# Weighing of heads, casts and last sums of the attention layer, in another order

## The chip, the cores and the metric

The kernel runs on one core of a Trainium2 chip. The metric is the device time of one execution in microseconds. Engines are named as in the profile: PE is TensorE (products), DVE is VectorE, ACT is ScalarE, POOL is GpSimd, SP is SyncE, whose queue issues the DMA transfers.

## The reference

One sequence of 1024 rows by 1024 columns goes through an mLSTM layer and then through a layer of dilated attention; the second one is what the change touches. Cut to that:

```python
def dilated_attention_layer(x, w_in, w_out, kv_blocks, slopes):
    proj = x @ w_in                                   # queries of 3 groups, 8 heads of 128; gate z
    for g, (window, dilation) in enumerate(GROUPS_B): # (128,1), (512,4), (2048,16)
        o, lse = dilated_block_attention(qb, kb, vb, dilation, window // dilation, slopes)
        ...
    wts = jax.nn.softmax(jnp.stack(lses), axis=0)     # over the three groups
    o = jnp.sum(wts[..., None] * jnp.stack(outs), axis=0)
    y = o * jax.nn.silu(z)
    return y @ w_out

x = layer_norm(ALPHA * x + y, ln_g, ln_b)
```

All is float32. A product is made of three products of a reduced type: each operand is split into a high part h and the rest l, and h·h, h·l and l·h are summed.

## The kernel before, in words

`split` (lines 91 to 93) makes such a pair: ScalarE casts the high part (92), VectorE subtracts it for the rest (93). `mm3` (95 to 99) issues the three products (97, 98, 99), each of 128x128 by 128x512. A scheduler orders each engine's instructions by a model of their times, in which the order of the text is a priority; within `issue_after(ins)` an instruction may not be issued ahead of `ins`. Each engine works through its own queue in order and waits by semaphores for the others. SBUF is cut into numbered slots (s0 to s52) of 128x1024, PSUM into eight banks (b0 to b7) of 128x512. How many buffers a small tile gets is decided by the compiler's own placement.

The attention layer runs two quads of four heads, in each the three groups, in each the four heads: `queries_keys` (products by Strassen's scheme, sums on VectorE in 224, 230, 260, 261), `scores` (1260, 1269 maximum, 1271 its negative, 1273 Exp on ScalarE), `attend` (1287 transposes, 1341 products with the values, 1349 copies). In the third group `factors` and `merge` (1383 to 1403) turn the three groups' maxima and denominators into weights, written to memory (df). `fetch` starts the loads of a head's three outputs and weights (1411 to 1415); `combine` multiplies and sums them (1424, 1426) and multiplies with the gate (1428). `weigh` calls it for a head, pinned behind the last `split`, and writes the result y. Before, head h is weighed after the attention of the next head. The last gates (`gates(3)`, 1473 and 1474) follow behind head 7's attention, and then heads 6 and 7's y.

The output projection has eight blocks c of 128 columns of y and rows of w_out; for each, y and w_out are loaded (1544, 1546) and split, blocks 6 and 7 straight from heads 6 and 7. `block` (line 1557 on) sums one block into a bank: a row tile tb of 128 rows has two halves dm, each 24 products in one bank. Tiles 0 to 3 are summed together; then tiles 4 to 7 one by one in banks b0 to b7, two each. `begin` loads the residual rows (1565) and, in `add_rows` (937 to 941), adds them to a bank (940) and takes statistics (941) half by half. `finish` aggregates (928, 930), computes the reciprocal root by an integer guess (357, 359) and three Newton steps of three instructions (361 to 363), the bias (1580), normalises on ScalarE (1582), and multiplies and adds gain and shift on VectorE (1583, 1584). `finish_last`, for tiles 6 and 7, centres and multiplies with the gain (1594) while no root is needed yet, and then multiplies with the root and adds the shift (1597); tile 7 does both in halves, and stores each half.

At the start, `setup` loads three gate weights in_wifr (449) into slot 51, one after another, and GpSimd multiplies and sums each (424 to 426); ScalarE copies the result (454).

## Time and profile before

| | us |
|---|---|
| three runs | 2020.54, 2025.85, 2025.57 |
| median of the three | 2025.57 |
| profiled execution, its own time | 2023.8 |
| its span, first to last instruction | 2022.0 |
| TensorE busy | 1969.0 (97%) |
| VectorE busy | 1451.8 (72%) |
| ScalarE busy | 1010.7 (50%) |
| GpSimd busy | 154.0 (8%) |

The profile is one execution. The span is what its instructions take from the first to the last; 1.8 us lie around it. The mean granted clock of TensorE over it is 0.996 of 2.4 GHz.

### The profile page before, as it was taken

To read this page: it belongs to the slowest core of one execution; us is meant where nothing else is said; L and a number is where in the kernel's file an instruction comes from. 1 tells how busy PE (TensorE), PEld (TensorE's weight loads), DVE (VectorE), ACT (ScalarE), POOL (GpSimd) and SP (SyncE) were. 2 spreads that over 40 slices of the span, in tenths; PEclk is the share of its full clock that TensorE was granted. 3 is DMA by queue.
4 is the path that set the end of the run, shared out by engine and by line. 5 is a ranking of instruction groups with operands and counts; after the bars stand their busy time and mean duration, and the time that the engine had idled before them with its cause. 6 is when DMAs were issued, how large, how long until landed. Compare 5 with 4: busy or idle time off the path is not lost. (4 is left out here: it accounts for less than half of the span.)

```text
span 2022.0 us, 26727 instructions
## 1 busy us (share of the span) xinstructions
PE 1969.0 (97%) x9576; PEld 1631.2 (81%) x9576; DVE 1451.8 (72%) x2867; ACT 1010.7 (50%) x2008; POOL 154.0 (8%) x127
## 2 busy tenths in 40 slices
PE   8999999999999999999999999999999999999897
PEld 6778888788888888878788888878877888888686
DVE  8778787675577776457867765776679877757878
ACT  5455555535645543343524542565554566765531
POOL 0110000012145343000000000000000000000000
PEclk9999999999999999999999999999999999999999
DMA  4345465456754543516121143224156322123753
GB/s 169 138 162 198 160 221 181 148 166 222 280 203 163 192 163 117 183 62 231 52 73 63 53 146 105 84 84 146 64 210 210 115 94 84 63 84 108 261 199 125
DMA packets 113148, 292.26 MB, mean 145 GB/s; under 512 B 13236, under 2 KB 31092, under 8 KB 113016
## 3 DMA queue, kind: packets, MB, share of 16 engines
q1 hardware_dynamic: 113016, 290.56, 41.1%
q8 instruction: 75, 1.23, 0.3%
q14 instruction: 57, 0.47, 0.1%
HBM read 202.13 MB, written 88.39 MB: 144 GB/s over the span
## 5 line engine op out<-in xcount | busy, mean ns | idle before, releaser
L98 PE MATMUL b<-s,s 128*128 128x512 f32 (+3 forms) x2720 | 1035.5, 382 | 3.0 <-DVE s L93 3.0
L97 PE MATMUL b<-s,s 128*128 128x512 f32 (+2 forms) x2720 | 1010.6, 386 | 28.0 <-ACT s L92 18.6
L99 PE MATMUL b<-s,s 128*128 128x512 f32 (+3 forms) x2720 | 1023.0, 383 | 4.9 <-DVE s L93 4.5
L92 ACT CAST s<-s 128x512 fp32r<-128x512 f32 (+3 forms) x706 | 436.5, 638 | 544.9 <-PE b L99 276.0
L93 DVE TENSOR_TENSOR s<-s,s 128x512 fp32r<-128x512 f32 (+3 forms) x702 | 508.2, 739 | 276.2 <-ACT s L92 272.6
L97 PEld LDWEIGHTS b<-s,s 128*128 128x128 f32 x2720 | 511.9, 188 | 134.6 <-ACT s L92 27.6
L99 PEld LDWEIGHTS b<-s,s 128*128 128x128 f32 x2720 | 511.1, 188 | 105.7 <-DVE s L93 10.2
L98 PEld LDWEIGHTS b<-s,s 128*128 128x128 f32 x2720 | 512.8, 189 | 99.3 <-DVE s L93 5.2
L230 DVE TENSOR_TENSOR s<-s,b 128x512 f32<-128x512 f32 x144 | 98.1, 682 | 37.8 <-PE b L99 35.6
L1273 ACT ACTIVATE s<-s,nmax 128x128 f32<-128x128 f32 (+1 forms) x192 | 84.3, 441 | 27.7 <-DVE nmax L1271 27.5
L224 DVE TENSOR_TENSOR s<-s,b 128x512 f32<-128x512 f32 x96 | 65.1, 680 | 19.9 <-PE b L99 16.4
L93 DVE TENSOR_TENSOR s<-b,s 128x512 fp32r<-128x512 f32 (+1 forms) x96 | 51.7, 553 | 33.9 <-ACT s L92 30.0
L558 DVE SCALAR_TENSOR_TENSOR s<-s,c_convw,s 128x512 f32<-128x512 f32 (+3 forms) x96 | 71.4, 755 | 3.1 <-ACT s L555 2.8
L802 ACT ACTIVATE s<-s,k 128x128 f32<-128x128 f32 x144 | 47.2, 392 | 42.2 <-DVE s L93 18.7
L243 DVE TENSOR_TENSOR s<-s,s 128x512 f32<-128x512 f32 x48 | 33.0, 688 | 42.9 <-DMA s<-in_w_xm 15.1
L1269 DVE CUSTOM_DVE_ANT_0 s<-b,k 128x128 f32<-128x128 f32 (+1 forms) x192 | 57.2, 346 | 3.5 <-PE b L99 3.2
L92 ACT CAST s<-b 128x512 fp32r<-128x512 f32 (+1 forms) x96 | 43.9, 480 | 21.9 <-PE b L99 14.5
L310 DVE TENSOR_TENSOR s<-s,s 128x1024 f32<-128x1024 f32 x32 | 40.1, 1253 | 20.1 <-DMA s<-in_w_o 9.9
L314 DVE TENSOR_TENSOR s<-s,b 128x512 f32<-128x512 f32 x80 | 50.7, 680 | 5.0 <-PE b L99 3.7
L1220 DVE SCALAR_TENSOR_TENSOR s<-s,s 128x512 fp32r<-128x512 f32 x48 | 42.3, 883 | 10.1 <-ACT s L1219 9.6
L761 POOL TENSOR_TENSOR s<-s 128x512 fp32r<-128x512 f32 x32 | 43.4, 1369 | 76.3 <-ACT s L760 68.8
L1287 PE MATMUL b<-c_ident,s 128*128 128x128 f32 x280 | 46.3, 277 | 2.0 <-ACT s L1273 1.9
(185 smaller groups left out, 1527.9 us busy)
## 6 DMA issues: line engine op xcount, KB each, us to landing
s<-in_w_qk SPq DMA_DIRECT2D x48, 512.0 KB
s<-in_w_out SPq DMA_DIRECT2D x40, 512.0 KB
dp<-s SPq DMA_DIRECT2D x32, 512.0 KB
s<-dp SPq DMA_DIRECT2D x32, 512.0 KB
s<-in_w_z SPq DMA_DIRECT2D x24, 512.0 KB
s<-in_w_v SPq DMA_DIRECT2D x24, 512.0 KB
dg<-s SPq DMA_DIRECT2D x24, 512.0 KB
s<-dg SPq DMA_DIRECT2D x24, 512.0 KB
```

What stands on the lines that cost most here:

```text
L92: self.nc.scalar.copy(h, src)
L93: self.last_split = (l_eng or self.nc.vector).tensor_tensor(l, src, f(h), op=ALU.subtract)
L97: mm(ps, lh, rh, start=start, stop=False, skip_group_check=skip)
L98: mm(ps, lh, rl, start=False, stop=False, skip_group_check=skip)
L99: mm(ps, ll, rh, start=False, stop=stop, skip_group_check=skip)
L224: V.tensor_tensor(o, p, q, op=add)
L230: V.tensor_tensor(o, p[lane][rows], q[lane][rows], op=add)
L314: V.tensor_tensor(o, p, q, op=add)
L558: V.scalar_tensor_tensor(u[i][:, lo:o + 512], xm[i][:, lo - s:o + 512 - s], convw[:, c, 3 - s:4 - s], u[i][:, lo:o + 512], op0=ALU.mult, o ...
L802: A.activation(E[:, i * P:i * P + P], src[:, i * P:i * P + P], AF.Exp, bias=self.bias[:, hd, ig, j:j + 1])
L1269: V.tensor_tensor_reduce(out=dst, in0=sc, in1=bias, op0=ALU.add, op1=ALU.max, scale=1.0, scalar=-3e38, accum_out=mx[:, b:b + 1])
L1273: self.last_exp = A.activation(res[b][0], res[b][0], AF.Exp, bias=nm[:, b:b + 1], accum_out=stat[:, 1, g, b:b + 1])
```

## The change

Three parts. **Weighing:** `weigh` is called from the middle of a `queries_keys` (or of `gates`) two heads later, behind the first of its steps, instead of after the next head's attention; heads 6 and 7's order behind a maximum or a split is written anew, and the slots of the sums are the same ring for both quads. **Casts:** the splits of the output projection's w_out and y (blocks 0 to 5 of y, all of w_out) may not issue ahead of the last Exp. **Last tiles:** the add of the second half of tiles 5, 6 and 7 may not issue ahead of the last VectorE operation of the tile before; tile 7's first half is centred on ScalarE (with a bias, minus the mean) and multiplied with the gain on GpSimd, instead of both on VectorE.

```diff
-    def add_rows(self, r, bs, ps, dm):
+    def add_rows(self, r, bs, ps, dm, behind=None):
...
-        V.scalar_tensor_tensor(r[:, ds], r[:, ds], ALPHA, ps, op0=ALU.mult, op1=ALU.add)
+        with self.tc.issue_after(behind.ins) if behind else ExitStack():
+            V.scalar_tensor_tensor(r[:, ds], r[:, ds], ALPHA, ps, op0=ALU.mult, op1=ALU.add)
...
-            self.strassen(self.quarters(a["w_qk"][g, h]), x, ones, None, done, V)
+            for n, _ in enumerate(self.strassen_steps(self.quarters(a["w_qk"][g, h]), x, ones, None, done, V)):
+                if n == 1:
+                    amid(h)
...
-        def weigh(h, fetched):
-
-            with self.tc.issue_after(self.last_split.ins):
+        def weigh(h, fetched, behind):
+
+            with self.tc.issue_after(behind.ins):
                 acc = combine(*fetched)
...
+        def weigh_late(h):
+
+            nonlocal late, merged, fourth
+            if not late or late[0] > h - 2:
+                return None
+            acc, late = weigh(*late, self.last_split if h < 8 else self.last_max), None
+            if merged == 3:
+
+                fourth = by_group(3, 50, 51, 52)
+            elif merged is not None:
+                late = fetch_late(merged)
+            merged = None
+            return acc
...
-            self.split(wh, wl, raw)
-            if c < 6:
-                self.split(yh, yl, f(yl))
-            else:
+            with self.tc.issue_after(self.last_exp.ins):
+                self.split(wh, wl, raw)
+                if c < 6:
+                    self.split(yh, yl, f(yl))
+            if c >= 6:
...
-            for ds in parts:
-                V.scalar_tensor_tensor(r[:, ds], r[:, ds], mv[:, 0, 0:1], gain[:, ds], op0=ALU.subtract, op1=ALU.mult)
+            if n == 2:
+
+                nm = self.t(self.cp, [P, 1], tag="lnb1", bufs=4)
+                V.tensor_scalar_mul(nm, mv[:, 0, 0:1], -1.0)
+                ds = parts[0]
+                A.activation(r[:, ds], r[:, ds], AF.Identity, bias=nm, scale=1.0)
+                G.tensor_tensor(r[:, ds], r[:, ds], gain[:, ds], op=ALU.mult)
+            ds = parts[-1]
+            V.scalar_tensor_tensor(r[:, ds], r[:, ds], mv[:, 0, 0:1], gain[:, ds], op0=ALU.subtract, op1=ALU.mult)
...
+        behind = None
         for tb in range(4, 8):
...
-            if tb < 6:
-                finish((tb,), [begin(tb, ps2)])
-            else:
-                finish_last(tb, begin(tb, ps2))
+            begun = begin(tb, ps2, behind)
+            behind = finish((tb,), [begun]) if tb < 6 else finish_last(tb, begun)
```

In the orders below, a name is the slot or bank with running numbers, outputs ahead of the arrow; line numbers after the change are a few higher than before (940 becomes 941, 1273 becomes 1276, 1390 becomes 1393, 1473 becomes 1476, 1583 becomes 1602, 1594 becomes 1621, 1597 becomes 1624).

ScalarE's queue at the last Exps, before; s4 and s6 are the first casts of the output projection (from the loads in s5 and s24), s41 and s42 casts of the last gates:

```order
L92 CAST s4_2761_16718<-s5_2762_16719 128x1024
L1390 ACTIVATE s36_2694_16258<-s36_2694_16258 8x384
L92 CAST s6_2759_16716<-s24_2758_16715 128x1024
L92 CAST s41_2749_16636<-s38_2738_16558 128x512
L92 CAST s42_2750_16654<-s39_2739_16560 128x512
L1273 ACTIVATE s48_2724_16464,stat_2186_13093<-s48_2724_16464,nmax_2725_16465 128x128 x4
L1473 ACTIVATE s32_2736_16556<-b0_2740_16562 128x512
L92 CAST s40_2751_16672<-s39_2739_16560 128x512
L92 CAST s24_2766_16729<-s25_2767_16730 128x1024
L1273 ACTIVATE s48_2724_16464,stat_2186_13093<-s48_2724_16464,nmax_2725_16465 128x128 x4
```

and after:

```order
L1393 ACTIVATE s36_2694_16258<-s36_2694_16258 8x384
L92 CAST s41_2749_16636<-s38_2738_16558 128x512
L92 CAST s42_2750_16654<-s39_2739_16560 128x512
L1276 ACTIVATE s48_2724_16464,stat_2184_13082<-s48_2724_16464,nmax_2725_16465 128x128 x8
L92 CAST s6_2759_16716<-s24_2758_16715 128x1024
L92 CAST s4_2761_16718<-s5_2762_16719 128x1024
L1476 ACTIVATE s32_2736_16556<-b0_2740_16562 128x512
L92 CAST s40_2751_16672<-s39_2739_16560 128x512
L1294 COPY s14_2732_16514<-b4_2733_16515 128x512
L92 CAST s24_2766_16729<-s25_2767_16730 128x1024
```

The two casts of the projection have moved from ahead of the Exps to behind them, and the gate's casts now come first.

VectorE's queue before, from the add of the last tile's first half (b6) to the add of its second (b7); s15 is tile 5, s37 tile 6, s46 tile 7, s43 the gain and s12 the shift:

```order
L940 SCALAR_TENSOR_TENSOR s46_2854_17380<-s46_2854_17380,b6_2852_17330 128x512
L362 SCALAR_TENSOR_TENSOR raw_2851_17316<-raw_2851_17316,ray_2850_17315 128x1
L1583 TENSOR_TENSOR s15_2837_17223<-s15_2837_17223,s43_2798_16805 128x1024
L941 BN_STATS lbs_2855_17382<-s46_2854_17380 128x6
L363 SCALAR_TENSOR_TENSOR ray_2850_17315<-raw_2851_17316,ray_2850_17315 128x1
L1584 TENSOR_TENSOR s15_2837_17223<-s15_2837_17223,s12_2799_16806 128x1024
L361 TENSOR_TENSOR raw_2851_17316<-ray_2850_17315,lx_2849_17312 128x1
L362 SCALAR_TENSOR_TENSOR raw_2851_17316<-raw_2851_17316,ray_2850_17315 128x1
L363 SCALAR_TENSOR_TENSOR ray_2850_17315<-raw_2851_17316,ray_2850_17315 128x1
L361 TENSOR_TENSOR raw_2851_17316<-ray_2850_17315,lx_2849_17312 128x1
L362 SCALAR_TENSOR_TENSOR raw_2851_17316<-raw_2851_17316,ray_2850_17315 128x1
L940 SCALAR_TENSOR_TENSOR s46_2854_17380<-s46_2854_17380,b7_2853_17331 128x512
```

and after, from the add of tile 5's second half (b3) past that of b6:

```order
L941 SCALAR_TENSOR_TENSOR s15_2837_17223<-s15_2837_17223,b3_2836_17174 128x512
L942 BN_STATS lbs_2838_17225<-s15_2837_17223 128x6
L928 BN_AGGR lmv_2839_17230<-lbs_2838_17225 128x2
L930 TENSOR_SCALAR lx_2840_17232<-lmv_2839_17230 128x1
L357 TENSOR_SCALAR ray_2841_17234<-lx_2840_17232 128x1
L941 SCALAR_TENSOR_TENSOR s46_2854_17380<-s46_2854_17380,b6_2852_17330 128x512
L359 ISA ray_2841_17234<-ray_2841_17234,magic_170_256 128x2
L942 BN_STATS lbs_2855_17382<-s46_2854_17380 128x6
```

then, behind nine Newton rows of tile 5, to the centring of tile 6:

```order
L1599 SCALAR_TENSOR_TENSOR lnb1_2843_17247<-lmv_2839_17230,ray_2841_17234 128x1
L1602 TENSOR_TENSOR s15_2837_17223<-s15_2837_17223,s43_2798_16805 128x1024
L1603 TENSOR_TENSOR s15_2837_17223<-s15_2837_17223,s12_2799_16806 128x1024
L941 SCALAR_TENSOR_TENSOR s37_2846_17303<-s37_2846_17303,b5_2845_17254 128x512
L942 BN_STATS lbs_2847_17305<-s37_2846_17303 128x6
L928 BN_AGGR lmv_2848_17310<-lbs_2847_17305 128x2
L930 TENSOR_SCALAR lx_2849_17312<-lmv_2848_17310 128x1
L1621 SCALAR_TENSOR_TENSOR s37_2846_17303<-s37_2846_17303,lmv_2848_17310,s43_2798_16805 128x1024
```

and, behind tile 6's guess and Newton rows, the add of b7 with what follows:

```order
L363 SCALAR_TENSOR_TENSOR ray_2850_17315<-raw_2851_17316,ray_2850_17315 128x1
L1624 SCALAR_TENSOR_TENSOR s37_2846_17303<-s37_2846_17303,ray_2850_17315,s12_2799_16806 128x1024
L941 SCALAR_TENSOR_TENSOR s46_2854_17380<-s46_2854_17380,b7_2853_17331 128x512
L942 BN_STATS lbs_2855_17382<-s46_2854_17380 128x6
L928 BN_AGGR lmv_2856_17387<-lbs_2855_17382 128x2
L930 TENSOR_SCALAR lx_2857_17389<-lmv_2856_17387 128x1
L1616 TENSOR_SCALAR lnb1_2858_17391<-lmv_2856_17387 128x1
L1621 SCALAR_TENSOR_TENSOR s46_2854_17380<-s46_2854_17380,lmv_2856_17387,s43_2798_16805 128x512
```

Before, the add of b7 has one row of tile 6's root and its last multiply-add behind it; now everything of tiles 5 and 6 stands ahead of it, and behind b6's add.

SyncE's queue at the gate weights, with its waits, before:

```order
L449 DMA s_261_847<-in_wifr 128x512 [waits DMAHW7_49,DMAHW2_49]
L531 DMA dz_29_94<-s_200_333 128x1024 [waits DMAHW0_49,Activation_49]
L449 DMA s_262_852<-in_wifr 128x512
L177 DMA s_307_1185<-in_w_xm 128x1024 [waits DVE_49]
L177 DMA s_308_1187<-in_w_xm 128x1024 [waits DMAHW3_49,DVE_49]
L449 DMA s_263_857<-in_wifr 128x512 [waits DMAHW4_49,Pool_49]
```

and after:

```order
L449 DMA s_261_847<-in_wifr 128x512 [waits DMAHW7_49,DMAHW2_49]
L531 DMA dz_29_94<-s_200_333 128x1024 [waits DMAHW0_49,Activation_49]
L449 DMA s_262_852<-in_wifr 128x512 [waits Pool_49]
L177 DMA s_307_1185<-in_w_xm 128x1024 [waits DVE_49]
L177 DMA s_308_1187<-in_w_xm 128x1024 [waits DMAHW3_49,DVE_49]
L449 DMA s_263_857<-in_wifr 128x512 [waits DMAHW4_49,Pool_49]
```

The second of the three loads of in_wifr has got a wait for GpSimd.

## Rows read from the trace of the kernel before

**Rows 1.** The page's first part: busy microseconds of each engine, its share of the span, and its instructions.

```profile
PE 1969.0 (97%) x9576; PEld 1631.2 (81%) x9576; DVE 1451.8 (72%) x2867; ACT 1010.7 (50%) x2008; POOL 154.0 (8%) x127
```

**Rows 2.** The list of waits, TensorE's longest: who waited for whom, microseconds in total, times, the longest.

```profile
PE b L97 <- ACT s L92: 18.6, 17, 6.2
```

**Rows 3.** The timeline of VectorE, 1901 to 1919 us: start, busy microseconds (to the end of the last instruction of the row), line, operation, and in brackets the idle time before it and what ended it. The nine pieces of work that the prediction speaks of lie between the last two rows.

```profile
1901.02 1.22 DVE L93 TENSOR_TENSOR s<-s,s 128x1024 fp32r<-128x1024 f32 x1
...
1905.72 0.67 DVE L224 TENSOR_TENSOR s<-s,b 128x512 f32<-128x512 f32 x1
1909.75 1.23 DVE L93 TENSOR_TENSOR s<-s,s 128x1024 fp32r<-128x1024 f32 x1 [3.36 <-ACT s L92]
...
1918.44 0.88 DVE L1402 TENSOR_TENSOR s<-s 8x128 f32<-8x128 f32 x3
```

**Rows 4.** The timelines of ScalarE and of TensorE round the same wait, with the same columns.

```profile
1908.67 2.09 ACT L92 CAST s<-s 128x1024 fp32r<-128x1024 f32 x3 [7.02 <-DMA s<-in_w_out]
1910.66 0.40 ACT L1273 ACTIVATE s<-s,nmax 128x128 f32<-128x128 f32 x1
...
1910.29 0.50 PE L97 MATMUL b<-s,s 128*128 128x512 f32 x1 [3.23 <-ACT s L92]
```

**Rows 5.** The stretches of 2 us from 1910 to 1916: start and end, length, busy time and instructions of TensorE, of its weight loads, of VectorE, ScalarE and GpSimd, then the granted clock of TensorE, the DMA engines' busy share and GB/s.

```profile
1910.00:1912.00 2.00, 1.60 (x6) 0.79 (x7) 2.00 (x5) 2.00 (x9) 0.00 (x0) 0.96 1.02 418
1912.00:1914.00 2.00, 2.00 (x6) 1.60 (x7) 2.00 (x5) 2.00 (x5) 0.00 (x0) 0.50 1.02 412
1914.00:1916.00 2.00, 2.00 (x7) 1.59 (x7) 2.00 (x5) 2.00 (x10) 0.00 (x0) 0.69 1.03 420
```

**Rows 6.** The chain of work that ended last, in order of time, 1949 to 1962 us: start, microseconds, what.

```profile
1949.05 1.37 DMA df<-s
...
1950.48 4.05 DMA s<-df
...
1954.56 1.29 DVE s L1424 x2
...
1961.47 0.63 ACT s L92
```

**Rows 7.** The timeline of TensorE, its wait for the y of head 7.

```profile
1962.14 0.50 PE L97 MATMUL b<-s,s 128*128 128x512 f32 x1 [0.22 <-ACT s L92]
```

**Rows 8.** Two stretches of 2 us behind idle times of TensorE elsewhere, columns as in rows 5.

```profile
1516.00:1518.00 2.00, 2.00 (x9) 1.62 (x8) 2.00 (x3) 1.05 (x2) 0.00 (x0) 0.50 0.06 19
1890.00:1892.00 2.00, 2.00 (x10) 1.65 (x9) 2.00 (x3) 1.90 (x3) 0.00 (x0) 1.00 0.05 18
```

**Rows 9.** The timeline of TensorE, the ends of those two idle times.

```profile
1514.81 0.50 PE L97 MATMUL b<-s,s 128*128 128x512 f32 x1 [1.98 <-DVE s L230]
...
1889.16 0.50 PE L97 MATMUL b<-s,s 128*128 128x512 f32 x1 [2.56 <-DVE s L230]
```

**Rows 10.** The timeline of TensorE, its last two products.

```profile
2010.78 0.39 PE L98 MATMUL b<-s,s 128*128 128x512 f32 x1
2011.01 0.39 PE L99 MATMUL b<-s,s 128*128 128x512 f32 x1
```

**Rows 11.** The timeline of VectorE, 2001 us to the end.

```profile
2001.90 0.14 DVE L1580 SCALAR_TENSOR_TENSOR lnb<-lmv,ray 128x1 f32<-128x1 f32 x1
...
2002.34 1.28 DVE L1594 SCALAR_TENSOR_TENSOR s<-s,lmv,s 128x1024 f32<-128x1024 f32 x1
...
2003.67 1.22 DVE L1583 TENSOR_TENSOR s<-s,s 128x1024 f32<-128x1024 f32 x1
...
2004.94 1.22 DVE L1584 TENSOR_TENSOR s<-s,s 128x1024 f32<-128x1024 f32 x1
...
2006.14 0.68 DVE L940 SCALAR_TENSOR_TENSOR s<-s,b 128x512 f32<-128x512 f32 x1
...
2011.44 0.69 DVE L940 SCALAR_TENSOR_TENSOR s<-s,b 128x512 f32<-128x512 f32 x1 [0.76 <-PE b L99]
...
2012.77 1.27 DVE L1597 SCALAR_TENSOR_TENSOR s<-s,ray,s 128x1024 f32<-128x1024 f32 x1
2013.95 0.20 DVE L928 BATCH_NORM_AGGREGATE lmv<-lbs 128x2 f32<-128x12 f32 x1
...
2015.58 0.15 DVE L357 TENSOR_SCALAR ray<-lx 128x1 int32<-128x1 int32 x1
...
2017.71 1.42 DVE L1597 SCALAR_TENSOR_TENSOR s<-s,ray,s 128x512 f32<-128x512 f32 x2
```

**Rows 12.** The timeline of ScalarE, the normalising of the tile before the last three.

```profile
2002.08 1.25 ACT L1582 ACTIVATE s<-s,lnb,ray 128x1024 f32<-128x1024 f32 x1 [18.68 <-DVE lnb L1580]
```

**Rows 13.** GpSimd's products of 128x512 elements by source line: least, median and longest duration in ns, first and last start in us, shapes.

```profile
L872 POOL TENSOR_TENSOR s<-s,s x32: 1272/1296/1736, 579.6 to 814.8; 128x512 f32<-128x512 f32 x32
```

**Rows 14.** The timelines of SyncE's queue, GpSimd, ScalarE and TensorE, 93 to 128 us.

```profile
93.44 0.46 SPq L449 DMA_DIRECT2D s<-in_wifr  x1
...
99.73 0.79 POOL L426 TENSOR_TENSOR k<-s 128x128 f32<-128x128 f32 x1
...
110.87 0.78 POOL L426 TENSOR_TENSOR k<-s 128x128 f32<-128x128 f32 x1
...
112.70 0.67 ACT L454 COPY s<-k 128x8 f32<-128x8 f32 x6
...
127.52 0.50 PE L97 MATMUL b<-s,s 128*128 128x512 f32 x1 [0.60 <-ACT s L92]
```

More of the change, by code (lines that the diff above doesn't have):

```diff
@@ L1495, in layer_b @@
                     self.w_raw = raw2
-                    for _ in gates(gate_at[quad, g], qk_slots[1::2]):
-                        pass
+                    for n, _ in enumerate(gates(gate_at[quad, g], qk_slots[1::2])):
+                        if n == 1:
+                            weigh_late(h + 1)
                 v = values(g, quad)
                 for h in heads:
-                    qk = queries_keys(h, g)
+                    qk = queries_keys(h, g, weigh_late)
                     p = scores(h, g, qk, stats[h])
-                    if h == 7 and late:
-                        y6, late = weigh(*late), None
+                    if h == 7 and g == 2:
+                        y6 = weigh_late(8)
                     if (quad, g) == (1, 0) and h < 7:
@@ L1561, in block, with begin @@
             self.mm3(ps, yh[:, ts], yl[:, ts], wh[:, ds], wl[:, ds], c == 0, c == HB - 1)
-        def begin(tb, ps2):
+        def begin(tb, ps2, behind=None):
             r = self.slot(rs)
@@ L1567, in begin @@
             for dm in range(2):
-                self.add_rows(r, bs, ps2[dm], dm)
+                self.add_rows(r, bs, ps2[dm], dm, behind if dm else None)
             return r, bs
@@ L1583, in finish @@
                 V.tensor_tensor(r, r, gain, op=ALU.mult)
-                V.tensor_tensor(r, r, shift, op=ALU.add)
+                last = V.tensor_tensor(r, r, shift, op=ALU.add)
                 store(tb, r)
+            return last
         def finish_last(tb, begun):
@@ L1592, in finish_last @@
             parts = [slice(D // n * i, D // n * i + D // n) for i in range(n)]
-            for ds in parts:
-                V.scalar_tensor_tensor(r[:, ds], r[:, ds], mv[:, 0, 0:1], gain[:, ds], op0=ALU.subtract, op1=ALU.mult)
+            if n == 2:
[6 more added lines that the diff above has]
+            V.scalar_tensor_tensor(r[:, ds], r[:, ds], mv[:, 0, 0:1], gain[:, ds], op0=ALU.subtract, op1=ALU.mult)
             rstd = self.rstd(x, 1, "ra")
             for ds in parts:
-                V.scalar_tensor_tensor(r[:, ds], r[:, ds], rstd, shift[:, ds], op0=ALU.mult, op1=ALU.add)
+                last = V.scalar_tensor_tensor(r[:, ds], r[:, ds], rstd, shift[:, ds], op0=ALU.mult, op1=ALU.add)
                 store(tb, r, ds)
+            return last
         pss = [[self.bank(2 * i + dm) for dm in range(2)] for i in range(4)]
```

25 lines of the change are left out of this document (12 added, 13 removed).

## The prediction

> **What bounds the kernel now.** I read the page's first part first: TensorE is busy 1969.0 us of a span of 2022.0 [rows 1], so a change can take time away only where TensorE stands still, or behind its last product. The list of waits says where it stands still: of all waits, those for ScalarE's casts (line 92) are the longest, 17 times and 18.6 us, one of them 6.2 [rows 2]. I then read the two places that the change touches, each on its own: the stretch round 1900 to 1962 us, and everything behind the last product.
>
> In the first place ScalarE stands idle 7.02 us, until 1908.67, in front of a cast of an output weight whose load has not landed [rows 4]. VectorE waits for that cast 3.36 us, until 1909.75 [rows 3], and TensorE 3.23 us, until 1910.29 [rows 4]; then the granted clock is 0.96, 0.50 and 0.69 in three stretches of 2 us [rows 5], the lower level (1.2 GHz) for part of that time, which costs 2 x (0.04 + 0.50 + 0.31) = 1.7 us. This looks like 4.9 us to be had. But the chain of waits shows what is late next: head 7's weights go out (1949.05) and come back (until 1954.54), are multiplied in, and the cast of its y starts at 1961.47 [rows 6]. TensorE waits only 0.22 us for it [rows 7]; it reaches that point only just too early, because it was held up before. In front of that chain VectorE is almost full, so it is VectorE's work ahead of it that sets its time.
>
> In the second place, TensorE's last product starts at 2011.01 and takes 0.39 [rows 10]. VectorE's add of the last bank starts at 2011.44, the first half of the last multiply-add at 2017.71, and the span ends at 2022.0 [rows 11]: 6.27 + 4.29 us that nothing hides.
>
> **The weighing.** By the order of instructions, no engine does heads 0 to 5 in another place; the text's new place for the weighing ends up where the scheduler had it. Cost: nothing, and nothing hides it or needs to.
>
> **The casts behind the last Exp.** What leaves ScalarE's and VectorE's queues there is the wait for the load. ScalarE now does the two gate casts and all eight Exps first, and then the cast s6. The maxima come at about 1906.7 (VectorE's row at 1905.72 in the old order, plus a half-width subtract and small rows), eight Exps of 0.39 end at 1909.9, and the cast of 1.05 ends at 1910.95. So VectorE's subtract s7 starts at 1910.95 instead of 1909.75: 1.2 us later. Ahead of it now stand nine pieces of work that came behind it, those between the rows at 1909.75 and 1918.44 and the latter (two gate subtracts and one Strassen sum of 0.60 each, head 6's merge with 0.30, 0.29, 0.13, 0.88 and 0.81, a maximum with 0.07): 4.28 us; one subtract of 1.13 (1901.02) went the other way [rows 3]. Net 3.15 us, less the 1.2: head 7's chain starts **1.95 us** earlier. Its bounds are 0.6 (the later output weights, whose loads now come no earlier, hold VectorE again) and 3.4 (all moved work and the idle time round it).
>
> TensorE would reach its wait for y7 at (1962.14 - 0.22) - 3.23 - 1.7 = 1957.0. The cast now lets it go at 1962.14 - 1.95 = 1960.2. The 3.23 us of idle time therefore come back as about 3.2 us in front of y7: the end moves by **-1.95 us**, not by -4.9. Does the clock fall again? After idle times of 3.23 us and 1.98 us the rows show 0.50; after one of 2.56 us they show 1.00 throughout [rows 5, 8, 9]. Two of three: I take it as more likely than not, **+1.65 us** if it falls, 0 if not.
>
> The Trainium skill ("TensorE: Matmul & The Clock Gate", Part 1, What's actually happening) says that the slow clock is the default and that activity releases it. By that rule an idle time that is only moved brings the fall along to its new place, and the sum is the one with 1.65; the row with 2.56 us and no fall is why I keep the other.
>
> **The sums in order by tile.** This is the costly part. The add of the second half of a tile now issues behind the last VectorE operation of the tile before it. On VectorE the add of b6 (first half of the last tile) still stands early, and it waits for TensorE: b6 is complete 24 products of 0.227 us, 5.45 us, before the end, at 2006.0. Behind this waiting instruction is queued nearly all of the finishing of tiles 5 and 6, which before ran ahead of and between these adds [rows 11], and behind that, in the same queue, the add of b7. Step by step from 2006.0, by distances between starts in [rows 11] and ScalarE's [rows 12] (a row's own duration is some 0.08 longer, since the next one starts before it is out): add b6 0.60, small 0.07, statistics 0.61, nine Newton steps of 0.195 1.76, nb 0.19, hand-over to ScalarE 0.18, its normalising 1.25, back 0.04, gain 1.13, shift 1.13 (tile 5); add b5 with its wait 0.72, statistics 0.73, aggregate 0.24, 0.07, centring 1.19, reciprocal root 2.13, last multiply-add 1.18 (tile 6). That is **13.2 us**: the add of b7 starts at 2019.2 instead of 2011.44, **+7.8 us**. TensorE is done all the while, so nothing covers this.
>
> Behind it the chain is shorter: add 0.72, statistics 0.73, aggregate 0.24, two small rows 0.14, half a centring 0.66, root 2.13 = 4.62 instead of 6.27: **-1.65 us** (tile 6's multiply-add of 1.18 no longer stands in it, and the other half of the centring is on ScalarE and GpSimd). That other half runs beside: ScalarE 0.18 + about 0.64 (the half of 1.25), GpSimd 1.27 to 1.74 by its products of this shape [rows 13], together 2.1 to 2.6 against VectorE's 0.07 + 0.66 + 2.13 = 2.86. Hidden, by 0.3 us; if it weren't, it would cost what exceeds that. The end: **+6.15 us**.
>
> The Trainium skill ("GPSIMD Engine Reference", Specifications) says that GpSimd's SBUF interfaces are shared with VectorE, with contention where VectorE reads two SBUF inputs. VectorE's half centring is such an instruction and stands beside that product; held for all of its 0.66, GpSimd would end 0.1 to 0.4 us late, and the sum would be 2031.3 at most.
>
> **A side effect at 93 to 128 us.** The buffers came out otherwise: the second load of the gate weights (line 449), issued at 93.44 before without a wait, now waits for GpSimd, whose work on the first ends at 100.5. The third load follows GpSimd's second round of some 3.3 us. GpSimd's last row there ended at 111.65 [rows 14]; by the shift of these loads I put it at 113.4. ScalarE's copies of the result, at 112.70, come 0.7 later; the casts queued behind them let TensorE go, which waits for one at 127.52 [rows 14], so there is no slack: **+0.7 us**, from 0 (ScalarE makes it up in idle time) to 1.5.
>
> **The sum**, against the profiled execution's own time of 2023.8 us: 6.15 - 1.95 + 1.65 + 0.7 = **+6.55 us** with a fall of the clock, +4.9 without. The profiled execution lies 1.8 below the median of the three runs (2025.57), and the middle of all four executions is 2024.7; I set the base between, at 2024.3: **2030.9** and 2029.2 us. What a measurement of this kernel can tell from no change is 0.3%, 6.1 us, so the forecast lies right at that bound.
>
> **The rivals.**
> - Head 7's chain takes all of it: y7 comes 4.9 us earlier, since the work that precedes it was held by the same load. 6.15 - 4.9 + 0.7 = +1.95: 2026.3 us. For it: its lateness at 1962.14 is small [rows 7]. Against: VectorE was waiting for 3.36 only, and 1.13 of work moved the wrong way [rows 3].
> - Head 7's chain gains nothing, since the later output weights hold VectorE instead; the clock falls, and the early wait costs 1.5: 6.15 + 1.65 + 1.5 = +9.3: 2033.6 us. For it: the loads stand in one queue whose order hardly changes. Against: head 6's merge, no load in it, is what moved ahead.
> - Faster: VectorE keeps up with TensorE at the end. The mechanism is the place of b6's add: if VectorE reached it with tiles 5 and 6 already finished, b7's add would start at 2011.44 as before and the chain behind it be 1.65 shorter. With y7 4.9 earlier and no price early that is -6.55: 2017.8 us. It decides at 13.2 us of work fitting into 5.45; since the order puts that work behind b6, I give it little.
> - The change doesn't do what it says: true of the weighing, as told, at no price; not of the other two parts, whose rows have moved.
>
> **How the numbers follow.** Forecast with a fall 0.40, without 0.30; all of the chain 0.12; nothing of it 0.13; faster 0.05. Faster by over 0.3%: 0.04, out of the last. Within: most of the forecast without a fall (0.25), a third of that with one (0.13), all of the first rival (0.12) and a hundredth of the last, 0.51. Slower by over 0.3%: 0.27 + 0.05 + 0.13 = 0.45. Within and slower hold nearly all; both are the same mechanism, cut by the bound. The range leaves out the faster case and the outer halves of the two rivals beside the forecast: 2026.0 to 2035.0; the likeliest case's own, by the bounds of y7 and of the early wait, is 2028.7 to 2033.1.
>
> **What would show it.** In the profile after: the add of b7 on VectorE starts 7 to 8.5 us behind TensorE's end, with tile 6's multiply-add right ahead of it; from there to the end some 8.9 us (4.62 + 4.29). TensorE has no long wait at 1907 to 1910, but one of 2 to 4.5 us, for the cast of y7, at about 1957 to 1960. The first part says 3.23 us of it moved, not vanished. Early, GpSimd waits for a load twice. I am wrong if b7's add starts within 2 us of TensorE's end, if y7's wait is under 1 us, or if heads 0 to 5 are weighed elsewhere in the trace.

## The result and the profile after

| | runs | median us | ratio to before, 95% interval |
|---|---|---|---|
| before | 9 | 2022.56 (2016.81 to 2025.85) | |
| changed kernel | 9 | 2030.95 (2029.23 to 2037.54) | 1.0043 [1.0031, 1.0054] |

The change costs 0.43%. The profiled execution of the changed kernel took 2029.23 us, its span is 2027.4. In larger sets of runs before's median came out at 2024.15 to 2024.42, so some of the 8.4 us between these two medians may be chance; what follows goes by ratios with their intervals, and by stretches of the traces.

**The page's first part and the list of waits** after, to be read beside [rows 1, 2]:

```profile
PE 1972.3 (97%) x9576; PEld 1637.4 (81%) x9576; DVE 1454.8 (72%) x2867; ACT 1012.5 (50%) x2009; POOL 155.1 (8%) x128
...
PE b L97 <- ACT s L92: 15.4, 12, 6.2
```

TensorE waits 3.2 us less for casts than before and is busy 3.3 us longer, and the stretches below show where part of that is products at the lower clock. What this wait lost is not a gain in time.

**The end.** The timeline of VectorE after, 2004 us to the end (columns as in [rows 11]):

```profile
2004.22 0.69 DVE L941 SCALAR_TENSOR_TENSOR s<-s,b 128x512 f32<-128x512 f32 x1 [0.94 <-PE b L99]
...
2008.76 1.22 DVE L1602 TENSOR_TENSOR s<-s,s 128x1024 f32<-128x1024 f32 x1 [1.31 <-ACT s L1601]
...
2016.23 1.28 DVE L1624 SCALAR_TENSOR_TENSOR s<-s,ray,s 128x1024 f32<-128x1024 f32 x1
2017.43 0.68 DVE L941 SCALAR_TENSOR_TENSOR s<-s,b 128x512 f32<-128x512 f32 x1
...
2020.09 0.16 DVE L359 CUSTOM_DVE_ANT_0 ray<-ray,magic 128x2 uint16<-128x2 uint16 x1
2020.29 1.16 DVE L361 TENSOR_TENSOR raw<-ray,lx 128x1 f32<-128x1 f32 x1
2021.48 0.16 DVE L362 SCALAR_TENSOR_TENSOR raw<-raw,ray 128x1 f32<-128x1 f32 x1
...
2023.11 1.42 DVE L1624 SCALAR_TENSOR_TENSOR s<-s,ray,s 128x512 f32<-128x512 f32 x2
```

And the timelines of TensorE (its last product) and of GpSimd in the same kernel:

```profile
2009.23 0.39 PE L99 MATMUL b<-s,s 128*128 128x512 f32 x1
...
2020.17 1.26 POOL L1619 TENSOR_TENSOR s<-s,s 128x512 f32<-128x512 f32 x1 [1207.34 <-ACT s L1618]
```

TensorE ends at 2009.23 + 0.39 = 2009.62. The add of b6 waits for it until 2004.22, and the add of b7 follows 13.21 us later, 7.81 us behind TensorE's end; before it stood 0.04 behind [rows 10, 11]. From b7's add to the end are 2027.4 - 2017.43 = 9.97 us (before 10.56). A row of 128 elements that takes 0.16 us elsewhere takes 1.16 at 2020.29, while GpSimd's product runs, and ends 0.02 behind it.

**The middle.** The timelines of ScalarE, of VectorE and of TensorE after, and the chain of waits:

```profile
1908.84 1.98 ACT L92 CAST s<-s 128x1024 fp32r<-128x1024 f32 x2
...
1909.90 1.23 DVE L93 TENSOR_TENSOR s<-s,s 128x1024 fp32r<-128x1024 f32 x1 [0.83 <-ACT s L92]
...
1958.76 0.50 PE L97 MATMUL b<-s,s 128*128 128x512 f32 x1 [2.22 <-ACT s L92]
...
1945.65 1.37 DMA df<-s
1947.04 4.13 DMA s<-df
...
1957.41 0.61 DVE s L1431
...
1958.09 0.63 ACT s L92
```

TensorE has no wait near 1907 us any more (before 3.23, [rows 4]) but one of 2.22 for y7's cast (before 0.22, [rows 7]). The stretches of 2 us behind it show the granted clock fall to the lower of its two levels, 1.2 GHz:

```profile
1958.00:1960.00 2.00, 1.24 (x4) 1.00 (x5) 1.87 (x4) 1.18 (x2) 0.00 (x0) 0.80 0.00 0
1960.00:1962.00 2.00, 2.00 (x6) 1.52 (x5) 0.03 (x1) 0.00 (x0) 0.00 (x0) 0.50 0.00 0
1962.00:1964.00 2.00, 2.00 (x9) 1.65 (x8) 0.00 (x0) 0.00 (x0) 0.00 (x0) 0.85 0.00 0
```

The clock falls once more in this trace, behind a wait of 2.98 us for line 230 near 1889, ahead of the first instruction that stands elsewhere after the change (a cast at 1899.9 before). Before, the wait of 2.56 there left it at 1.00 [rows 8, 9]:

```profile
1888.53 0.79 PE L97 MATMUL b<-s,s 128*128 128x512 f32 x1 [2.98 <-DVE s L230]
...
1890.00:1892.00 2.00, 2.00 (x6) 1.61 (x5) 2.00 (x4) 1.11 (x3) 0.00 (x0) 0.50 0.02 3
```

Sixty products on, TensorE is 13.93 us behind that wait (before 12.97). It comes to its wait for y7 0.95 us later after 1889 than in the other three kernels with the casts moved as here, which shortens that wait by as much.

**The start.** The timelines of SyncE's queue, GpSimd, ScalarE and TensorE after, to be read beside [rows 14]:

```profile
99.90 0.33 SPq L449 DMA_DIRECT2D s<-in_wifr  x1
105.45 0.33 SPq L449 DMA_DIRECT2D s<-in_wifr  x1
...
102.58 1.49 POOL L424 TENSOR_TENSOR s<-s,s 128x512 f32<-128x512 f32 x1 [2.71 <-issue]
...
108.06 1.08 POOL L424 TENSOR_TENSOR s<-s,s 128x512 f32<-128x512 f32 x1 [1.07 <-DMA s<-in_wifr]
...
111.17 0.69 ACT L454 COPY s<-k 128x8 f32<-128x8 f32 x6 [1.58 <-POOL k L426]
...
123.69 0.50 PE L97 MATMUL b<-s,s 128*128 128x512 f32 x1 [0.62 <-ACT s L92]
...
125.01 0.40 PE L599 MATMUL b<-s,k 128*16 128x512 f32 x1 [0.59 <-ACT s L92]
126.02 0.63 PE L97 MATMUL b<-s,s 128*128 128x512 f32 x1 [0.60 <-ACT s L92]
...
126.00:128.00 2.00, 1.98 (x7) 1.79 (x8) 2.00 (x6) 1.49 (x3) 0.00 (x0) 0.56 0.36 102
128.00:130.00 2.00, 2.00 (x6) 1.56 (x6) 1.98 (x5) 0.37 (x1) 0.00 (x0) 0.59 1.06 317
```

The second load now goes out at 99.90 instead of 93.44, and GpSimd stands idle 2.71 and 1.07 us in front of its work on the two later loads. ScalarE waits 1.58 us for GpSimd, and TensorE waits three times in a row for casts (0.62, 0.59, 0.60; before twice, 0.48 and 0.60). The last two rows are stretches of 2 us behind that, with a granted clock of 0.56 and 0.59; before all stretches there had 1.00.

### The profile page after: what moved, and what is told of

The parts are those of the page before. It is cut to its first block, busy times and chain, and to the rows that moved or that the text cites. A ratio compares the mean times of both kernels' runs of the same rounds, so it can differ in the third digit from the quotient of the medians.

```text
span 2027.4 us, 26736 instructions
## 1 busy us (share of the span) xinstructions
PE 1972.3 (97%) x9576; PEld 1637.4 (81%) x9576; DVE 1454.8 (72%) x2867; ACT 1012.5 (50%) x2009; POOL 155.1 (8%) x128
## 4 chain that ended last, share of the span: by engine, by line
PE 76%; DVE 9%; DMA 5%; ACT 3%; issue 2%; SPq 0%; POOL 0%; DVEq 0%; ACTq 0%
PE b L97 23%; PE b L99 23%; PE b L98 23%; DVE s L93 2%; PE b L593 1%; DMA s<-df 1%; PE b L1290 1%; DMA df<-s 1%; ACT s L92 1%; PE b L599 1%; PE b L868 1%; DMA s<-in_w_qk 1%; DMA s<-in_w_out 1%; PE b L1313 1%; DVE s L1427 0%
```

## The experiments

TensorE's end is called T below. The table reads four places in each trace: TensorE's wait near 1907 to 1917 for the cast of an output weight, its wait for y7's cast, the time from the wait for line 230 near 1889 ([rows 9]) to T, and from T to the end of the span.

| kernel | wait near 1910 | wait for y7 | granted clock 0.50 in a stretch of 2 us behind either | 1889 to T | T to end |
|---|---|---|---|---|---|
| before | 3.23 | 0.22 | yes | 122.24 | 10.60 |
| changed | none | 2.22 | yes | 121.09 | 17.78 |
| casts alone | none | 3.74 | yes | 122.53 | 10.58 |
| order by tile alone | 1.49 | 1.30 | no | 120.17 | 17.37 |
| tile 7 split alone | 3.14 | none | yes | 122.02 | 11.05 |
| weighing alone | 1.21 | 0.92 | no | 119.42 | 10.65 |
| casts, merge ahead | none | 0.98 | no | 117.34 | 10.58 |
| merge ahead alone | 0.95 | 0.72 | no | 118.97 | 10.66 |
| changed, both halves pinned | none | 3.06 | yes | 122.05 | 15.76 |
| two products on GpSimd | 2.92 | none | yes | 121.93 | 11.95 |
| tile 7's second add alone | 2.77 | 0.23 | yes | 121.23 | 10.19 |
| casts, merge ahead, slot 46 | none | none | no | 116.34 | 10.62 |
| changed, slot 46 | none | 3.69 | yes | 122.73 | 17.86 |
| best of all | none | 0.21 | no | 116.53 | 10.19 |

Each row is one execution. Six of these kernels (before, order by tile, tile 7 split, weighing, two products, tile 7's second add) have the same order of instructions on every engine up to 1995 us, and on TensorE to the end. Their first four columns are therefore six executions of one and the same thing: from 1889 to T they take 119.42 to 122.24, mean 121.17, and before's is the longest. The four with the casts moved as in the change (changed, casts alone, both halves pinned, changed with slot 46) take 121.09 to 122.73, mean 122.10.

The clock falls to the lower level behind the wait near 1889, too, in nine of the fourteen. This hardly counts in the fifth column: sixty products on, the five without a fall stand 12.95 to 12.99 us behind the wait, and seven of the nine with one 12.97 to 12.99 (the changed kernel 13.93, tile 7 split 13.37). In the five TensorE waits 1.15 to 1.16 us for a cast on the way; the nine show no wait over 0.5 there.

### Each part alone

**Casts alone.** Only the splits behind the last Exp.

```diff
+            with self.tc.issue_after(self.last_exp.ins):
+                self.split(wh, wl, raw)
+                if c < 6:
+                    self.split(yh, yl, f(yl))
```

> The kernel before with only the splits of the output projection pinned behind the last Exp. The prediction's steps, added up: y of head 7 comes 1.95 us earlier (2.75 by the trace after), the clock falls there (+1.65), the early wait of the second gate-weight load costs 0 to 1.5: in all -1.1 to +1.2 us, within what can be told from no change. In its trace TensorE has no long wait at 1907 to 1910, but one of 2 to 3 us for the cast of y7, with a granted clock of 0.5 behind it. Rival (the stall is truly recovered): -4.9 us, no wait at y7. The second load of in_wifr should wait for GpSimd here if this part is what brought that about.

Measured: 2026.72 us (12 runs) beside 2024.42, ratio 1.0010 [0.9997, 1.0023]. No gain: the wait of 3.23 is gone, one of 3.74 stands in front of y7, and the clock falls behind it as before. The timeline of TensorE:

```profile
1962.40 0.79 PE L97 MATMUL b<-s,s 128*128 128x512 f32 x1 [3.74 <-ACT s L92]
```

The early wait is there too (ScalarE 1.80 us): it comes with this part.

**Order by tile alone.** Only the pin of the second halves' adds; tile 7 is centred on VectorE as before.

```diff
-                self.add_rows(r, bs, ps2[dm], dm)
+                self.add_rows(r, bs, ps2[dm], dm, behind if dm else None)
```

> The kernel before with only the order of the last tiles (the second half's add of tiles 5, 6, 7 behind the last operation of the tile before); tile 7's centring stays on VectorE. Theory (VectorE's serial finishing sets the end): b7's add starts 7.8 us behind TensorE's end, and from there 9.5 us to the end of the span (10.6 before, less tile 6's multiply-add of 1.18, with 0.1 of other waits): +6.7 us, 2029 to 2030 against a before of about 2022.6. The Newton row that took 1.16 us in the trace after should take 0.16 here, since GpSimd does nothing. Rival (that row was not GpSimd's doing): it takes about 1.2 here too and the total is +7.7.

Measured: 2031.03 us (12), 1.0031 [1.0019, 1.0042]. This part alone is most of the loss. The timeline of VectorE has b7's add 7.81 us behind T (2008.53), as in the changed kernel, and the row of line 361 that took 1.16 there takes 0.16 here, with no GpSimd product beside it:

```profile
2003.13 0.69 DVE L941 SCALAR_TENSOR_TENSOR s<-s,b 128x512 f32<-128x512 f32 x1 [0.70 <-PE b L99]
...
2016.34 0.68 DVE L941 SCALAR_TENSOR_TENSOR s<-s,b 128x512 f32<-128x512 f32 x1
...
2019.80 0.16 DVE L361 TENSOR_TENSOR raw<-ray,lx 128x1 f32<-128x1 f32 x1
```

**Tile 7 split alone.** The first half's centring on ScalarE and its gain on GpSimd.

```diff
+                A.activation(r[:, ds], r[:, ds], AF.Identity, bias=nm, scale=1.0)
+                G.tensor_tensor(r[:, ds], r[:, ds], gain[:, ds], op=ALU.mult)
```

> The kernel before with only tile 7's first half centred on ScalarE and multiplied with the gain on GpSimd. Theory (GpSimd's product holds a VectorE row that reads two SBUF operands until it is done): half a centring of 0.66 leaves VectorE, a small row of 0.07 comes, one Newton row lasts about 1.1 instead of 0.16: +0.4 us in the tail, so no difference that can be measured. Rival (they run side by side): -0.6 us, Newton rows of 0.16 throughout.

Measured: 2023.63 us (12), 0.9993 [0.9981, 1.0006]: nothing that can be told. In the trace the tail is 0.45 longer, not shorter, since VectorE saves 0.66 and then stands 1.0 at a row of line 361.

**Weighing alone.** Only the calls of `weigh_late`.

```diff
+                if n == 1:
+                    amid(h)
```

> The kernel before with only the new place of the weighing in the text. Theory (its instructions stand in the same order): 0.0 us, within 0.3%, and the same waits as before. Rival (the part of the measured difference that the two profiled executions do not show, some 3 us, lies here): +3 us.

Measured: 2024.26 us (12), 0.9997 [0.9985, 1.0010]. Nothing: on every engine the instructions stand in the order of before. Its trace is therefore a second execution of before, and it shows what the landing of one load makes of the same program: ScalarE's cast of that output weight starts 17.47 us behind the wait near 1889 instead of 19.51, and TensorE waits 1.21 instead of 3.23, with no fall of the clock. The four parts add up to 0.10 + 0.31 - 0.07 - 0.03 = 0.31%, against 0.43% [0.31, 0.54] for the whole.

### The end

**Both halves pinned.** The changed kernel, with the add of the first half behind the tile before as well. VectorE then doesn't stand at b6's add with tiles 5 and 6 queued behind.

```diff
-                self.add_rows(r, bs, ps2[dm], dm, behind if dm else None)
+                self.add_rows(r, bs, ps2[dm], dm, behind)
```

> The changed kernel, but with both halves' adds of tiles 5 to 7 behind the last operation of the tile before, so that the add of b6 no longer stands ahead of tile 5's finishing and holds it. If the wait of b6's add is what costs (as the prediction put it): b7's add starts no more than 2 or 3 us behind TensorE's end, and most of the 6 us comes back. If it is the finishing of the tiles one behind another, with VectorE idle at each hand-over to ScalarE and each dependent Newton row: tiles 4, 5 and 6 in series end 16.6 us behind 1998, b7's add starts 5 to 6 us behind TensorE's end, 0.6 more lies behind it for the first half's statistics, and the time is 1 to 2 us below the changed kernel: 2029 to 2030.

Measured: 2032.40 us (5), 1.0054 [1.0035, 1.0073]. No gain in time, where 1 to 2 us were expected; the end itself is 15.76 us instead of 17.78. In the two traces that gain is used up ahead of it: about 1.0 us from 1889 to T (its wait for y7 is 3.06), and the rest ahead of 1889, where both run the same order. T is 2011.94, and VectorE's timeline has both adds of tile 7 4.75 us behind it:

```profile
2006.95 1.22 DVE L1602 TENSOR_TENSOR s<-s,s 128x1024 f32<-128x1024 f32 x1 [1.31 <-ACT s L1601]
...
2015.48 1.28 DVE L1624 SCALAR_TENSOR_TENSOR s<-s,ray,s 128x1024 f32<-128x1024 f32 x1
2016.69 1.28 DVE L941 SCALAR_TENSOR_TENSOR s<-s,b 128x512 f32<-128x512 f32 x2
```

So the wait of b6's add is worth about 2.0 us of the tail, net of the first half's add and statistics, which now stand behind it; the rest stays without it. It is the order itself: one tile's chain after the other, with 1.31 us of idle time at the hand-over to ScalarE and Newton rows 0.195 apart. Before, rows of three tiles filled these gaps [rows 11].

**Tile 7's second add alone.** Before, with the pin for that one add.

```diff
+            begun = begin(tb, ps2, behind if tb == 7 else None)
```

> The kernel before with the add of b7 alone (the last tile's second half) behind tile 6's last operation; tiles 5 and 6 as before, and tile 7's centring on VectorE. Theory: tile 6's last multiply-add of 1.18 leaves the last chain, b7's add starts 0.6 to 0.7 us behind its bank, and from TensorE's end to the end of the span it is 9.9 to 10.1 us instead of 10.6: 0.5 to 0.7 us gained, not to be told from no change by the times. Rival (any order by tile costs): above 10.6.

Measured: 2025.46 us (10), 1.0007 [0.9996, 1.0018]. In the trace the tail is 10.19 instead of 10.60: tile 6's multiply-add no longer stands behind b7's add. 0.4 us is too little for these runs.

**Two products on GpSimd.** Tile 7 split, with the product on GpSimd done twice, first into a spare slot; this is more work than the kernel needs.

```diff
+                extra = self.slot(47)
+                G.tensor_tensor(extra[:, ds], r[:, ds], gain[:, ds], op=ALU.mult)
```

> e3 with GpSimd's product done twice: first into a spare tile that nobody reads, then in place as in e3 (the output is unchanged). Theory (a VectorE row that reads two SBUF operands and starts while GpSimd's product runs is held until that product is done): two of the Newton rows behind the half centring are held, 0.8 to 1.2 us each instead of 0.16, or one for more than 2 us, and from TensorE's end to the end of the span it is 12.0 to 12.4 us instead of 11.05. Rival (the one long row has to do with something else, such as the first row behind the guess): one long row of 1.16 as in e3, the others 0.16, 11.1 to 11.4 us.

Measured: one execution of each, 2023.99 us beside 2028.24, with no interval; it is read by its trace. The timelines of VectorE and of GpSimd:

```profile
2014.01 0.16 DVE L359 CUSTOM_DVE_ANT_0 ray<-ray,magic 128x2 uint16<-128x2 uint16 x1
2014.20 1.16 DVE L361 TENSOR_TENSOR raw<-ray,lx 128x1 f32<-128x1 f32 x1
2015.40 0.16 DVE L362 SCALAR_TENSOR_TENSOR raw<-raw,ray 128x1 f32<-128x1 f32 x1
2015.59 1.11 DVE L363 SCALAR_TENSOR_TENSOR ray<-raw,ray 128x1 f32<-128x1 f32 x1
2016.74 0.16 DVE L361 TENSOR_TENSOR raw<-ray,lx 128x1 f32<-128x1 f32 x1
...
2014.09 1.26 POOL L1600 TENSOR_TENSOR s<-s,s 128x512 f32<-128x512 f32 x1 [1199.65 <-ACT s L1598]
2015.43 1.26 POOL L1601 TENSOR_TENSOR s<-s,s 128x512 f32<-128x512 f32 x1
```

Two products, two held rows. The products end at 2015.35 and 2016.69, the rows at 2015.36 and 2016.70; the row that fits between them takes 0.16. The tail is 11.95, 0.9 longer than with one product.

### The middle and the start

**Casts, merge ahead.** Casts alone, with the splits of blocks 6 and 7 (w_out and y6) pinned behind the last product of head 7's merge, so that they can't stand ahead of it on VectorE.

```diff
+            with self.tc.issue_after((self.last_exp if c < 6 else self.last_merge).ins):
...
+                    with self.tc.issue_after(self.last_merge.ins):
+                        self.split(yh[:, cs], yl[:, cs], y[c - 6][:, cs])
```

> The kernel before with the casts behind the last Exp as in the change, and besides the casts of blocks 6 and 7 (w_out and y) pinned behind the last product of head 7's merge, which moves some 3.5 us of casts from ahead of that merge to behind it. Theory (what the stall at 1907 to 1910 gave back was lost again in front of head 7's y, and then on the clock): y7 comes 3.5 to 4.5 us earlier than with the casts alone, TensorE's wait for it (2.2 and 3.7 us in the traces so far) is at most 0.5 us, the granted clock stays at 1.00 there, and the time is 4 to 6 us below the casts alone: 1.5 to 5 us below the kernel before. Rival (the next late thing is the cast of block 6, or another load): TensorE waits for that instead, and the time is that of the casts alone, about 2 us above the kernel before.

Measured: 2023.80 us (11) beside 2024.18, 1.0000 [0.9989, 1.0011]. From the wait near 1889 to T it takes 117.34 us: 5.2 less than casts alone, and 4.9 less than before's trace, but 3.8 less than the mean of the six executions of before's order. TensorE waits only 0.98 for y7, and the clock does not fall behind it:

```profile
1958.02 0.50 PE L97 MATMUL b<-s,s 128*128 128x512 f32 x1 [0.98 <-ACT s L92]
```

But the early wait is in it too, and the time as a whole shows no gain, where 1.5 to 5 us were expected.

**Merge ahead alone.** That pin without the casts behind the last Exp.

```diff
+            with self.tc.issue_after(self.last_merge.ins) if c >= 6 else ExitStack():
+                self.split(wh, wl, raw)
```

> The kernel before with only the pin of e5: casts of blocks 6 and 7 behind head 7's merge, the other casts where they were. Theory: TensorE's wait for y7 (0.2 to 1.3 us in the traces of that order) goes, and nothing else: 0.2 to 1.3 us below the kernel before, not to be told from no change; the stall at 1907 to 1910 (1.2 to 3.2 us) stays. Rival (head 7's chain is not what counts in this order either way): 0.0.

Measured: 2022.61 us (11), 1.0005 [0.9991, 1.0019]. Nothing that can be told. From 1889 to T it takes 118.97 us, a little below what the other kernels with the casts in their old place show (119.42 to 122.24); with the casts moved as well it takes 117.34. The wait for y7 is 0.72 and not gone, as was expected.

**Slot 46.** Casts, merge ahead, with the second gate weight loaded into another slot, so that its load needn't wait for GpSimd.

```diff
-            rep = self.slot(51, (P, NC_A, 4, 8))
+            rep = self.slot((51, 46, 51)[i], (P, NC_A, 4, 8))
```

> e5 (casts behind the last Exp, blocks 6 and 7 behind head 7's merge), and the second of the three gate-weight loads (in_wifr) goes into slot 46 instead of 51, so that it doesn't wait for GpSimd's work on the first. Theory (the early wait is dearer than the 0.7 us of the prediction, since ScalarE waits 1.6 to 2.1 us for GpSimd at 111 us and TensorE's clock falls at 126 to 130 us): the three wait-free loads give 1.7 to 3.5 us back against e5, no granted clock below 0.9 between 120 and 132 us, and the time is 2 to 4 us below the kernel before. Rival (what ate the gain of e5 lies elsewhere): the time stays that of e5.

Measured: 2020.07 us (12) beside 2024.15, 0.9978 [0.9967, 0.9989]: faster than before, where the same kernel with the early wait stood at 1.0000. The second load goes out at 96.02 and the third, in the same row, at about 101. The clock stays up where it had fallen, as two stretches of 2 us show:

```profile
96.02 5.24 SPq L449 DMA_DIRECT2D s<-in_wifr  x2
...
126.00:128.00 2.00, 2.00 (x11) 1.63 (x10) 2.00 (x5) 0.24 (x2) 0.00 (x0) 1.00 0.93 201
128.00:130.00 2.00, 2.00 (x13) 1.76 (x12) 0.43 (x1) 0.53 (x1) 0.00 (x0) 1.00 0.83 299
```

The other slot does more than take the new wait away. The third load has to wait only for GpSimd's work on the first, and goes out 2 us earlier than before (103.02). So part of what this kernel gains on before lies at the start (1.3 us, by the comparison below) and has nothing to do with the casts.

**Changed, slot 46.** The same line in the changed kernel.

> The changed kernel with the same other slot for the second gate-weight load, all else as in the change. Theory: of its 8 to 9 us over the kernel before, the early wait is 1.7 to 3.5: the time is 5 to 7 us over the kernel before (ratio 1.0025 to 1.0035). Rival (the early wait is covered): ratio 1.004 or more, as the changed kernel.

Measured: 2034.16 us (10), 1.0042 [1.0028, 1.0055]. The start's saving doesn't show in the time, where a ratio of 1.0025 to 1.0035 was expected. The trace has it: at 148 us it is 2.3 us ahead of the changed kernel's. From there to 1889 it takes 4.9 us longer, in a stretch that takes 1739.9 to 1748.0 us in the fourteen traces, and from 1889 to T 1.6 longer (3.69 of wait for y7). Whether chance does that or the earlier start, these runs don't settle.

**Best of all.** Slot 46 with casts and merge ahead, and the pin of tile 7's second add.

```diff
+                self.add_rows(r, bs, ps2[dm], dm, behind if dm else None)
...
+            begun = begin(tb, ps2, behind if tb == 7 else None)
```

> e9 and, of the order by tile, only the add of the last tile's second half behind tile 6's last operation (e8). Theory: from TensorE's end to the end of the span 10.2 us as in e8, 0.4 below e9, the rest as in e9: 2.5 to 4.5 us below the kernel before. Rival (the parts aren't additive): no faster than e9 by its trace's last stretch, 10.6.

Measured: 2015.89 us (6, 2013.87 to 2017.72) beside 2024.15, 0.9960 [0.9947, 0.9972]. It beats both kernels: 0.40% below before and, worked out from the two ratios, 1 - 0.9960 / 1.0043 = 0.83% below the changed one. That is more than its parts: 2.5 to 4.5 us below before were expected, and 8.3 were measured, 4.2 below the kernel without the pin, of which the pin's 0.4 in the tail is a tenth. The two traces differ by 1.1 us only (spans 2013.8 and 2014.9), so the rest has no cause that these runs show.

## Why the prediction was right

The forecast was 2030.9 us and the median is 2030.95. That closeness is luck: the base of 2024.3 was not that of these runs (2022.56), and the terms are off by more. The prediction gave 0.51 to a time within 0.3% of before and 0.45 to a slower one; it came out slower, by 0.43% [0.31, 0.54]. What it had right is the mechanism: the order at the end costs most, and the wait of the casts only moves.

- **Weighing: nothing.** Right (0.9997).
- **b7's add 7.8 us later.** Right to the step: 13.21 us measured between the adds of b6 and b7 against 13.2 added up, T + 7.81. The words "behind this waiting instruction" told only part of why. The kernel with both halves pinned has no such wait and still stands at T + 4.75: the larger part is that the tiles' chains no longer fill each other's gaps.
- **The chain behind it 1.65 shorter.** Mis-sized. It is 0.59 shorter (9.97 against 10.56). The step that failed is "hidden, by 0.3 us; if it weren't, it would cost what exceeds that". GpSimd's product ends in time, but it holds the VectorE row that starts beside it, and that row is on the chain: 1.16 - 0.16 = 1.0 us. The remark drawn there from the Trainium skill ("GPSIMD Engine Reference", Specifications: SBUF interfaces shared with VectorE, contention where VectorE reads two SBUF inputs) named the right cause and took the wrong victim: it held GpSimd for VectorE's centring. The trace shows GpSimd's 1.26 us undisturbed and VectorE's row held, and the kernel with two products shows it twice. The trace of before had it already: a row of line 362 took 1.26 us at 563.06 while GpSimd's line 810 ran from 562.55 to 564.30. The timelines of VectorE and GpSimd before:

```profile
563.06 1.26 DVE L362 SCALAR_TENSOR_TENSOR raw<-raw,ray 128x4 f32<-128x4 f32 x1
...
562.55 1.75 POOL L810 TENSOR_TENSOR s<-s,s 128x512 f32<-128x512 f32 x1 [7.74 <-DVE raw L361]
```

The tail came to 17.78 - 10.60 = +7.18, forecast 6.15.
- **y7's chain 1.95 earlier, the idle time moved.** Right in kind. Counted from the wait near 1889, y7's cast starts 2.75 us earlier in the changed kernel (1958.09 - 1888.53 against 1961.47 - 1889.16) and 2.2 with casts alone, within the bounds of 0.6 and 3.4. But before's is the latest of six executions of its order, 69.5 to 72.3 us behind the wait near 1889, mean 71.2; the four kernels with these casts moved have 69.4 to 70.1, mean 69.8. On the mean that is 1.4 us, and the ranges overlap. TensorE's idle time came back as 2.22 (casts alone 3.74), as forecast for 2 to 4.5.
- **The fall of the clock, +1.65.** Right: ten products behind the wait for y7 took 3.98 us, from 1958.76 to 1962.74, instead of 10 x 0.227 = 2.27, so 1.7. The rule of the Trainium skill quoted there ("TensorE: Matmul & The Clock Gate", Part 1, What's actually happening), that the slow clock is the default and activity releases it, agrees with the 0.50 at 1960 to 1962. That idle time which is moved brings the fall along was the prediction's own step, and it held in all four kernels with these casts.
- **Both together, -0.30.** Mis-sized. In the pair of profiled executions 1889 to T gives -1.15. But what was credited to removing the wait near 1910 was one execution's: in the seven traces where these casts stand as before, it is 0.95 to 3.23 us, by when the load lands. By the means under the table the four kernels with the casts moved take 122.10 - 121.17 = 0.9 us more, not less.
- **The early wait, +0.7, at most 1.5.** Mis-sized. Comparing the same products over the traces (their starts against the mean of all, change from 81 to 148 us), four kernels with the wait lose 0.5 to 2.0 us, mean 1.4; seven without it lie between -1.3 and +1.0, mean -0.2; three with slot 46 gain 1.4 to 1.6. That is about 1.6 us for the wait. The forecast followed the casts as far as TensorE's first wait; it did not see that three waits of 0.6 in a row can be followed by the lower clock (0.56 and 0.59). Three of the four have that fall and lose 1.6 to 2.0; both halves pinned has the same three waits with the clock at 1.00 throughout, and loses 0.5.

With the sizes of the pair the sum is 7.18 - 1.15 + 1.6 = 7.6 us, against 6.55 on record; with the means for the middle it is 7.18 + 0.9 + 1.6 = 9.7. The medians differ by 8.4, and the interval of the ratio is 6.3 to 10.9 us, so neither sum is ruled out. The spans of the two profiled executions differ by 5.4, 2.2 less than the first sum. Up to 81 us the changed one is 0.5 ahead; from there to 148 it loses 0.6 and not 1.6, since before's execution is itself 1.0 behind the mean there; from 148 to 1889, where the order of instructions is the same, it gains 0.7. I have no cause for that but the spread of single executions.

The rivals: "all of it" fell, since y7 came 2.75 earlier at the most. "Nothing of it" is not ruled out as clearly: its +9.3 lies within the interval, VectorE does stand 1.32 us for the cast of a later output weight (up to 1918.44 in the changed kernel), and y7 came earlier against the mean of the six executions, but not against the earliest of them. What came lies between that rival and the forecast. The faster case fell at the order of VectorE, as told.

**Where the gain of the casts went** is the other question, since a wait of 3.23 us was removed. It did not lie on the path: head 7's merge, and the trip of its weights to memory and back (1945.65 to 1951.2 in the chain above), let y7 go, and VectorE's splits of blocks 6 and 7 stood ahead of that merge. With them pinned behind it and the casts moved, y7's cast starts 66.4 to 67.4 us behind the wait near 1889 in three traces, 3.0 earlier on the mean than with the casts moved alone, and the time to T is 116.34 to 117.34 against 121.09 to 122.73. Some 1.6 us of that gain was lost at the start, in a wait that the same edit brought along 1,800 us earlier. The 2 us or so that should remain for casts, merge ahead lie within its interval (2.2 us either way). All four kernels with the casts moved and slot 51 have it and none of the seven with the casts in place; why the program comes out so, by the placement of buffers or otherwise, is not shown.

## What to carry to other kernels

When you remove a wait, follow the chain to what comes next and move that as well, or the idle time only changes its place and takes the fall of the clock along. An order by tile at the end costs what the tiles' chains had filled in for each other: pin only the last add, not every one (0.4 us better by its trace, which the times can't tell). A wait for a load that is read from one trace is one execution's; read it in several before you price it. After an edit, compare the first waits of each load queue with those before, even far from the edit, since buffers may have been placed otherwise.

## What the runs showed of the hardware that was not expected

- A VectorE row of 128x1 with two SBUF inputs that starts while a GpSimd product of 128x512 runs ends with that product: 1.16, 1.16 and 1.11 us instead of 0.16, ending 0.01 to 0.02 behind it.
- The granted clock fell to 0.50 behind single waits of 2.22 to 3.74 us for the two casts of the table in eight of these traces, and not behind waits of 0.72 to 1.49. Near 1889 it fell behind waits of 2.01 to 4.58 us in nine traces, and stayed at 1.00 behind 1.55, 1.71, 1.96, 2.56 and 2.65 in the five others; so the length of the wait alone did not decide it. At the start, three waits of about 0.6 us close together were followed by a fall in three kernels, and not in a fourth.
- A fall of the clock need not cost time: near 1889 seven traces with one are as far sixty products on (12.97 to 12.99 us) as five without (12.95 to 12.99).
- When a load of output weights lands differs from one execution to the next by enough to move TensorE's wait for it between 0.95 and 3.23 us, in seven traces; six of them run the same order of instructions up to there and beyond.
